# A list scheduler's table of durations is rewritten, and its rule for picking the next piece is widened

## The chip, the cores and the metric

The kernel runs on one core of one Trainium2 chip. The metric is device time in microseconds from one launch to its end, as the median of several executions. One further execution was taken with the hardware profiler; all rows below come from it.

## The reference

Two layers of an encoder over 1024 tokens of width 1024. In each layer one wide projection of `x` (1024 to 11520 columns) feeds three mixers, and their gated sum goes through an output projection and a layer norm:

```python
for l in range(DEPTH):
    h = jnp.einsum('bsd,dn->bsn', x, w_in[l]) + b_in[l]
    (u_a, z_a, p_b, z_b, q_c, k_c, v_c, z_c, g_a, g_b, g_c) = _split(h, SPLIT_SIZES)
    o_a = rwkv7_branch(u_a, z_a, ...)      # a recurrence over the tokens, 16 heads, both directions
    o_b = pool_branch(p_b, z_b, ...)
    o_c = attention_branch(q_c, k_c, v_c, z_c, cos, sin)
    merged = (sigmoid(g_a) * (o_a @ proj_a[l]) + sigmoid(g_b) * (o_b @ proj_b[l])
              + sigmoid(g_c) * (o_c @ proj_c[l]))
    x = _normalize(DEEPNORM_ALPHA * x + merged @ w_out[l], LN_EPS) * ln_g[l] + ln_b[l]
```

The recurrence of the first mixer is, for every head and token, `state = state * w + (state @ nkk) b + v k` with output `state @ r`. The kernel does it in chunks of 64 tokens, which turns it into small matrix products, a 64 by 64 triangular inverse for each chunk, and a chain from chunk to chunk.

## The kernel before, in words

**Dense work.** Every large product is done in float32 accuracy by splitting both operands into a high and a low part. One piece (`mm` in `Dense.make`) is three matmuls of 128x512 for one slice k of the sum: L584, L585 and L586, written "a dense triple" below. A tile of the projection is 8 slices times 2 halves of the tokens. A weight block of four slices is loaded by SP, cast to its high part by ScalarE (L552, `wh`) and split into its low part by GpSimd (L553, `wl`).

**The recurrent stage** (`rwkv`). Heads are worked off in 8 pairs j, each in 4 quarters q, so 32 quarters a layer. In a quarter, both directions of 4 chunks are prepared together:
- `prep` (`fac1` to `fac3`, `score`): scaled copies of keys and queries. `fac3` makes one half of `nk` on GpSimd (L965) and scales it on VectorE (L967, L968); `score` is L979 on TensorE, masked by VectorE (L982, L984).
- `inverse`: a serial chain of levels. Each is 16 or 32 small matmuls in quarters of the array (L1053), then one VectorE operation (`X`, L1085) and one ScalarE cast (`U`, L1086), on which the next level's matmuls wait. GpSimd makes a low part for it (L1065).
- `seq`: four steps a quarter, each A, then B, then C, and then the next step's A. A is L1142 and L1144 on TensorE, then `u` on VectorE (L1148); B is L1159, then two copies on ScalarE (`uv`, L1163); C is L1173 and L1178, then the state's update `sbd` (L1183) and an output copy `y` (L1188 or L1190) on VectorE.
- Further pieces: `nkt` (L1009), `av` (L1023), the low-rank products (`psl`, L911 and L912), the norm of the keys (`psk` L782, `psr` L824), the output norm (`psy`, L1244).

The attention stage transposes each v tile (`psv`, L1431) after ScalarE has evacuated it (`rawv`, L1367).

**What sets the order.** The whole program is written out in the order that a list scheduler (`Sched.run`) makes while the kernel is built. Each piece of work is a `Th` with a list of steps (engine, ns). The scheduler keeps a clock for each engine, works out for the next piece of each line when it could begin (`st`), and takes, of those that begin within `TOL` of the earliest, the one with the lowest `p`; `p` is a due time, or the place of the line. On TensorE a piece's `st` holds a margin `LATE` of 146 ns after its operands. Dense triples of the recurrent stage come from a `Feed`; they have the highest `p`, so they fill in, unless the scheduler's own account of the clock asks for them. Every engine runs its instructions in the order in which they are written, so this list alone decides who stands behind whom:

```python
st = r if e == "W" else max(ck[e], r + (HOPI + LATE if e == "P" else 0.0))
...
lim = min(c[0] for c in cand) + TOL
st, p, r, ln = min((c for c in cand if c[0] <= lim), key=lambda c: c[1])
```

The durations are never read on the chip. They only shape the order.

Of the kernel before, what the change touches and what calls it, by code (L numbers as in the profile page):

```python
# [20 lines left out]
DEPTH, S, D = 2, 1024, 1024  # L21
# [78 lines left out]
SLACK, RESERVE, LATE, TOL, BUB = 1112.0, 20000.0, 146.0, 26.0, 87.0  # L100
# [15 lines left out]
class Th:  # L116
# [4 lines left out]
    __slots__ = ("fn", "steps", "needs", "gives", "ring", "chain", "rows", "side", "hold", "drop", "tail", "gen", "due", "lag")  # L121

    def __init__(self, fn, steps, needs=(), gives=(), ring=(), chain=True, rows=0.5, side=(), hold=None, drop=None, tail=None, lag=0.0):
# [4 lines left out]
        self.due, self.lag = None, lag  # L128
# [8 lines left out]
class Feed:  # L137
# [10 lines left out]
    def work(self):  # L148
        return 640.0 * self.n
# [33 lines left out]
class Sched:  # L183
# [3 lines left out]
    def __init__(self):  # L187
# [6 lines left out]
        self.dense = False  # L194
        self.hist = []

    def pe(self, start, ns, rows):
# [5 lines left out]
        t = start + ns * f  # L203
# [37 lines left out]
    def step(self, ln, steps, t, rows):  # L241

        for ops in steps:
            end = 0.0
            for e, ns, more, early in ops:
# [3 lines left out]
                else:  # L249
                    x = max(x, self.clock[e])  # L250
                    y = self.pe(x, ns, rows) if e == "P" else x + ns
# [7 lines left out]
    def issue(self, ln, r):  # L259
# [22 lines left out]
        ln.t = self.step(ln, steps, ln.t, th.rows)  # L282
# [101 lines left out]
def trunk(ctx: ExitStack, tc: tile.TileContext, a: dict, out, dbg=None):  # L384
# [124 lines left out]
    class Dense:  # L509
# [56 lines left out]
        def make(self, src, nk, rhs, evac, halves=(0, 1), needs=(), gives=(), ev=(("A", 570.0),), key=None, ering=(), first=False):  # L566
# [62 lines left out]
    def rwkv(l):  # L629
        P = pc["P"]  # L630
        w_in = a["w_in"][l]
        with ExitStack() as es:
# [110 lines left out]
            def pair_uv(j):  # L743
                o = []

                def tr(o, tg):
# [3 lines left out]
                    def fn():  # L750
# [13 lines left out]
                return ([Th(tr(0, t0), [("P", 428.0), ("A", 530.0), ("A", 530.0)], needs=n0 + [("v", j)], ring=("m",), gives=[("uv0", j)])],  # L764
                        [Th(tr(1, t1), [("P", 428.0), ("A", 530.0), ("A", 530.0)], needs=n1, ring=("m",), gives=[("uv", j)])])
# [3 lines left out]
            def pair_kk(j):  # L769
# [73 lines left out]
                for g in range(2):  # L843
                    o += [Th(f2(g), [("A", 520.0)], needs=[("kt", j)], ring=("t",), hold=hold[g]),
                          Th(f4(g), [("P", 428.0), ("D", 660.0)], ring=("m",), drop=hold[g])]
                o.append(Th(f5, [("G", 3770.0)]))
# [45 lines left out]
            def prep(j, d, q):  # L892
# [96 lines left out]
                if q % 2 == 0:  # L989
# [4 lines left out]
                      Th(score, [("P", 980.0), ("D", 602.0), ("D", 602.0)], needs=ss, ring=("m", "m"), gives=[("sc", d, Q)])]  # L994
# [3 lines left out]
            def joint(j, q):  # L998
# [28 lines left out]
                return ([Th(nkt, [("P", 930.0), ("A", 500.0), ("A", 500.0)], needs=[("sc", d, Q) for d in range(2)], ring=("m", "m"), gives=[("nkt", Q)])],  # L1027
# [959 lines left out]
```

## Time and profile before

| | |
|---|---|
| Median of 3 runs | 4210.23 us (4204.23 to 4212.84) |
| The profiled execution | 4213.04 us, span of its instructions 4211.3 us |
| Mean granted TensorE clock | 0.984 of full |
| TensorE busy | 4072.7 us, 97% of the span |
| VectorE, ScalarE, GpSimd busy | 2358.1, 2057.1, 1650.8 us |
| Dense matmuls L584, L585, L586 on `xh` | 3136 each, mean 425, 395, 396 ns |

Matmuls are pipelined, so the time from one matmul's start to the next one's start is less than the duration that a row gives. Where the text speaks of a slot, it is that distance between starts.

### The profile page before, as it was taken

Reading aid. Unit: us, or ns where it says so; the run is one execution under the profiler, and the core shown is the slowest. Engines: PE = TensorE matmul, PEld = TensorE weight load, DVE = VectorE, ACT = ScalarE, POOL = GpSimd, SP = SyncE. Lnnn points to the kernel's source line nnn. Section 1 sums busy time; section 2 is a strip of 40 time slices with the busy share of each in tenths; the row PEclk is TensorE's granted clock in tenths of the full one; section 3 lists DMA queues with packets and bytes.
Section 4 is the critical chain, followed back from the end, with each engine's and each line's share of the span. In section 5 each row is a group of like instructions: output and inputs, shape, how many; then the busy total and the mean of one; then the engine's idle time right before and its main releaser. Section 6 shows DMA issues by size and latency. Waiting matters only on the chain. (4 is left out here: it accounts for less than half of the span.)

```text
span 4211.3 us, 118890 instructions
## 1 busy us (share of the span) xinstructions
PE 4072.7 (97%) x50808; PEld 3195.4 (76%) x50808; DVE 2358.1 (56%) x4361; ACT 2057.1 (49%) x4198; POOL 1650.8 (39%) x2498
## 2 busy tenths in 40 slices
PE   8999999999999999999989999999999999999998
PEld 6777777777777778877767777777777777788777
DVE  3766666565504555545647666665655046555455
ACT  5566666565523553322146666665655235533210
POOL 4344334443343333353243443444433333333532
PEclk9999999999999899999999999999999999999999
DMA  2111111111134333155311111111111343321553
GB/s 90 33 42 36 44 40 37 41 36 50 48 101 111 116 109 98 55 174 190 121 51 32 38 39 42 40 36 44 34 53 48 106 113 112 115 88 55 180 182 118
DMA packets 329185, 326.30 MB, mean 77 GB/s; under 512 B 23536, under 2 KB 264384, under 8 KB 328655
## 3 DMA queue, kind: packets, MB, share of 16 engines
q1 hardware_dynamic: 301551, 233.66, 18.7%
q0 software_dynamic: 27104, 85.04, 5.8%
q8 instruction: 398, 6.52, 0.6%
q14 instruction: 132, 1.08, 0.1%
HBM read 224.86 MB, written 81.99 MB: 73 GB/s over the span
## 5 line engine op out<-in xcount | busy, mean ns | idle before, releaser
L584 PE MATMUL psdn<-xh,wh 128*128 128x512 f32 x3136 | 1332.1, 425 | 12.6 <-ACT wh L552 10.5
L586 PE MATMUL psdn<-xh,wl 128*128 128x512 f32 x3136 | 1241.4, 396 | 8.4 <-POOL wl L553 7.9
L585 PE MATMUL psdn<-xl,wh 128*128 128x512 f32 x3136 | 1238.5, 395 | 0.0
L553 POOL TENSOR_TENSOR wl<-wr,wh 128x512 fp32r<-128x512 f32 (+1 forms) x436 | 587.3, 1348 | 1222.1 <-ACT wh L552 1212.0
L584 PEld LDWEIGHTS psdn<-xh,wh 128*128 128x128 f32 x3136 | 596.2, 190 | 174.0 <-issue 27.6
L586 PEld LDWEIGHTS psdn<-xh,wl 128*128 128x128 f32 x3136 | 595.2, 190 | 151.3 <-POOL wl L553 17.8
L585 PEld LDWEIGHTS psdn<-xl,wh 128*128 128x128 f32 x3136 | 598.3, 191 | 105.3 <-issue 6.9
L552 ACT CAST wh<-wr 128x512 fp32r<-128x512 f32 (+2 forms) x484 | 291.3, 602 | 674.9 <-PE psdn L585 279.6
L1085 DVE TENSOR_TENSOR X<-pst,c 128x512 f16<-128x512 f32 x320 | 219.7, 687 | 191.8 <-PE pst L1053 185.7
L1086 ACT CAST U<-pst 128x512 f16<-128x512 f32 x320 | 185.9, 581 | 95.2 <-PE pst L1053 91.8
L1183 DVE SCALAR_TENSOR_TENSOR sbd<-sqp,wc,sbd 128x64 f32<-128x64 f32 x480 | 114.2, 279 | 203.7 <-PE sqp L1178 179.1
L1163 ACT COPY uv<-sqp 64x128 f32<-64x128 f32 x512 | 133.0, 260 | 97.5 <-PE sqp L1159 87.8
L1152 ACT ACTIVATE sbd<-sbd,wc 128x64 f32<-128x64 f32 x480 | 140.9, 343 | 61.9 <-PE sqp L1144 61.6
L1065 POOL TENSOR_TENSOR nl<-sc,nh 64x512 f16<-64x512 f32 x128 | 156.2, 1220 | 16.9 <-ACT nh L1062 11.4
L979 PE MATMUL pssc<-ar,nk 64*64 64x128 f32 x4096 | 150.7, 274 | 1.5 <-ACT uv L759 1.4
L1148 DVE TENSOR_TENSOR u<-sqp,sc 128x128 f32<-128x128 f32 x256 | 73.8, 288 | 136.7 <-PE sqp L1144 78.7
L625 POOL DMA_DIRECT2D sga<-gt x96 | 54.1, 564 | 245.0 <-ACT gt L624 134.1
L965 POOL TENSOR_TENSOR nk<-ta,k 128x256 f32<-128x256 f32 x128 | 98.0, 766 | 132.0 <-ACT ta L958 128.4
L1053 PEld LDWEIGHTS <-X 64*64 64x64 f16 x6144 | 130.0, 110 | 23.2 <-DVE sc L984 6.4
L1159 PEld LDWEIGHTS sqp<-u,sc 64*64 64x64 f32 x2048 | 79.6, 133 | 82.5 <-issue 42.4
L1053 PEld LDWEIGHTS <-U 64*64 64x64 f16 x5120 | 112.6, 109 | 36.6 <-ACT uv L1163 13.7
L1053 PE MATMUL pst<-X,U 64*64 64x64 f16 x5120 | 137.3, 194 | 1.0 <-ACT U L1086 0.7
(717 smaller groups left out, 8021.4 us busy)
## 6 DMA issues: line engine op xcount, KB each, us to landing
wr<-in_w_in_dram SPq DMA_DIRECT2D x360, 256.0 KB, 3.0
sga<-gt POOLq DMA_DIRECT2D x96, 256.0 KB, 2.3
g<-sga SPq DMA_DIRECT2D x96, 256.0 KB, 4.4
wr<-in_proj_a_dram SPq DMA_DIRECT2D x64, 256.0 KB, 3.1
sza<-sz POOLq DMA_DIRECT2D x32, 256.0 KB, 3.6
bva<-bv POOLq DMA_DIRECT2D x32, 256.0 KB, 4.0
oa<-o POOLq DMA_DIRECT2D x32, 256.0 KB, 3.6
oat<-oa SPq DMA_DIRECT2D x32, 256.0 KB, 4.2
```

The source lines that it names most:

```text
L552: nc.scalar.copy(hi[:, 0:n, :], r[:, 0:n, :])
L553: self.lo.tensor_tensor(out=lo[:, 0:n, :], in0=r[:, 0:n, :], in1=hi[:, 0:n, :], op=ALU.subtract)
L584: nc.tensor.matmul(ps, lhsT=hi[:, kk, :], rhs=ah, start=(k == 0), stop=False)
L585: nc.tensor.matmul(ps, lhsT=hi[:, kk, :], rhs=al, start=False, stop=False)
L586: nc.tensor.matmul(ps, lhsT=lo[:, kk, :], rhs=ah, start=False, stop=(k == nk - 1))
L979: nc.tensor.matmul(ps[h][HS[h if x == 0 else 1 - h], c, :], lhsT=nk[HS[h], c, x, :], rhs=ar[HS[h], c].rearrange("p a t -> p (a t)"), start ...
L1053: nc.tensor.matmul(ps[hs, d, c], lhsT=l, rhs=r, start=start and d == 0 and c == 0, stop=stop, skip_group_check=True)
L1065: nc.gpsimd.tensor_tensor(out=nl[HS[h]], in0=sc[HS[h], :, :, h, 0:64], in1=nh[HS[h]], op=ALU.subtract)
L1085: tt(out=x, in0=ps[0], in1=mask(i + 1), op=ALU.mult)
L1086: nc.scalar.copy(L["U"], ps[1])
L1152: act(sbd[d], sbd[d], AF.Copy, scale=J["wc", d, Q % NB][:, pl[d][0]:pl[d][0] + 1])
L1163: nc.scalar.copy(uv[HS[h], two, h, :], pu[HS[h], 128:256].rearrange("p (s e) -> p s e", s=2))
```

## The change

Three things are changed in the scheduler's numbers; no operation of the kernel is added or taken away.

1. The durations of the pieces: a dense triple is booked at 690 ns instead of 640, the side work that it triggers at 520 ns on ScalarE instead of 307 and 1235 ns on GpSimd instead of 620, the matmuls of an inverse level at 560 instead of 1000 ns, and so on.
2. A piece can have a shape (`full`, `quarters`, `columns`, `rows`); the scheduler's TensorE clock takes `SWITCH` = 92 ns more when the shape differs from the piece before.
3. `TOL` is 200 ns instead of 26.

```diff
-SLACK, RESERVE, LATE, TOL, BUB = 1112.0, 20000.0, 146.0, 26.0, 87.0
+SWITCH, PROD = 92.0, 690.0
+SLACK, RESERVE, LATE, TOL, BUB = 1112.0, 20000.0, 146.0, 200.0, 87.0
...
-        t = start + ns * f
+        t = start + (ns + (SWITCH if shape != self.shape else 0.0)) * f
+        self.shape = shape
...
-                        out_.append(Th(mm(pi, kk, h), [("P", 640.0)],
-                                       side=(("A", 307.0), ("G" if self.lo is nc.gpsimd else "D", 620.0 if self.lo is nc.gpsimd else 335.0)) if kk == 0 and h == halves[0] else (),
+                        out_.append(Th(mm(pi, kk, h), [("P", PROD)],
+                                       side=(("A", 520.0), ("G" if self.lo is nc.gpsimd else "D", 1235.0 if self.lo is nc.gpsimd else 602.0)) if kk == 0 and h == halves[0] else (),
...
-                    inv.append(Th(levx(i), [("P", 1000.0), [("D", 690.0), ("A", 600.0)]] if i < 5 else [("P", 540.0), ("D", 690.0)], rows=RI))
+                    inv.append(Th(levx(i), [("P", 560.0), [("D", 602.0), ("A", 480.0)]] if i < 5 else [("P", 290.0), ("D", 602.0)], rows=RI, shape="quarters"))
```

The changed file is four lines longer, so its lines have numbers that are higher by 4 (L1148 becomes L1152). The order moves over the whole program. The places that the prediction speaks of are shown from it.

**TensorE, pair 6, first quarter, second step**, from the last dense matmul ahead of B to C. `sqp` is the step's PSUM tile, `u` what VectorE made after A, `uv` what ScalarE makes after B. Before (the left-out rows are two inverse levels, and the second dense triple):

```order
L586 MATMUL psdn<-xh,wl 128x512
L1159 MATMUL sqp<-u_17891,sc 64x64 x4
...
L584 MATMUL psdn<-xh,wh 128x512
L585 MATMUL psdn<-xl,wh 128x512
...
L1173 MATMUL sqp<-uv,nk 64x64 x4
L1178 MATMUL sqp<-uv,sc 64x64 x4
```

The same step in the changed order:

```order
L590 MATMUL psdn<-xh,wl 128x512
L1163 MATMUL sqp<-u_17205,sc 64x64 x4
L983 MATMUL pssc<-ar,nk 64x128 x16
L1177 MATMUL sqp<-uv,nk 64x64 x4
L1182 MATMUL sqp<-uv,sc 64x64 x4
L588 MATMUL psdn<-xh,wh 128x512
```

Between B and C there were two inverse levels and two dense triples; now there is one half of a score, and TensorE goes back to dense work only behind C.

**VectorE, the same place**, from the state update ahead of A to `u`. Before:

```order
L1183 SCALAR_TENSOR_TENSOR sbd_295<-sqp,wc,sbd_295 128x64
L1188 COPY y<-sqp 128x2x64
L967 SCALAR_TENSOR_TENSOR nk<-nk,cum 128x4x64
L968 TENSOR_TENSOR nk<-nk,cum 128x4x64
L1085 TENSOR_TENSOR X<-pst_17778,c_284 128x512
L1148 TENSOR_TENSOR u_17891<-sqp,sc 128x128
```

In the changed order the next `u` of that quarter stands so:

```order
L1187 SCALAR_TENSOR_TENSOR sbd_295<-sqp,wc,sbd_295 128x64
L1192 COPY y<-sqp 128x2x64
L988 TENSOR_TENSOR sc<-pssc,c_284 128x4x128
L950 TENSOR_TENSOR ar<-kk,lw 128x4x63
L953 TENSOR_TENSOR ar<-r,lw 128x4x64
L1152 TENSOR_TENSOR u_17324<-sqp,sc 128x128
```

Where `u` stood behind the scaling of `nk`, whose second instruction reads what GpSimd makes, it now stands behind a masked score and two products that GpSimd has no part in.

## Rows read from the trace of the kernel before

**Rows 1.** Busy time by stretch: us, engines, granted clock, DMA share, GB/s.

```profile
130.00:1160.00 1030.00, 1022.22 (x20497) 785.73 (x20496) 656.31 (x1413) 649.88 (x1415) 423.02 (x804) 1.00 0.13 40
...
2235.00:3175.00 940.00, 927.81 (x18546) 712.74 (x18539) 614.94 (x1310) 600.54 (x1299) 394.53 (x760) 1.00 0.13 40
```

**Rows 2.** Waits of TensorE: us in total, times, longest us.

```profile
PE psr L824 <- ACT nx L797: 11.8, 2, 5.9
...
PE sqp L1159 <- DVE u L1148: 8.5, 9, 2.4
...
PE psv L1431 <- ACT rawv L1367: 3.6, 2, 2.0
```

**Rows 3.** Timeline of TensorE: start us, us, engine, line, operation.

```profile
601.30 0.39 PE L585 MATMUL psdn<-xl,wh 128*128 128x512 f32 x1
...
602.23 0.40 PE L586 MATMUL psdn<-xh,wl 128*128 128x512 f32 x1
602.56 0.44 PE L1053 MATMUL pst<-T,nh 64*64 64x64 f16 x16
...
604.33 0.50 PE L584 MATMUL psdn<-xh,wh 128*128 128x512 f32 x1
604.67 0.39 PE L585 MATMUL psdn<-xl,wh 128*128 128x512 f32 x1
...
609.64 0.22 PE L1144 MATMUL sqp<-sbd,ar 64*64 64x64 f32 x1
609.79 0.70 PE L871 MATMUL psb<-rk__10834,cst 128*128 128x512 f32 x1
```

**Rows 4.** Timeline of TensorE where only dense triples are left.

```profile
1194.80 0.39 PE L584 MATMUL psdn<-xh,wh 128*128 128x512 f32 x1
...
1203.41 0.39 PE L586 MATMUL psdn<-xh,wl 128*128 128x512 f32 x1
```

**Rows 5.** Timeline of VectorE, pair 6.

```profile
952.01 0.97 DVE L967 SCALAR_TENSOR_TENSOR nk<-nk,cum 128x256 f32<-128x256 f32 x1
955.66 0.43 DVE L968 TENSOR_TENSOR nk<-nk,cum 128x256 f32<-128x256 f32 x1 [2.68 <-POOL nk L965]
...
956.60 0.28 DVE L1148 TENSOR_TENSOR u<-sqp,sc 128x128 f32<-128x128 f32 x1
```

**Rows 6.** Timeline of GpSimd, same stretch.

```profile
952.77 1.36 POOL L553 TENSOR_TENSOR wl<-wr,wh 128x512 fp32r<-128x512 f32 x1
...
954.89 0.74 POOL L965 TENSOR_TENSOR nk<-ta,k 128x256 f32<-128x256 f32 x1
```

**Rows 7.** Timeline of TensorE, same stretch.

```profile
954.16 0.39 PE L586 MATMUL psdn<-xh,wl 128*128 128x512 f32 x1
956.94 0.45 PE L1159 MATMUL sqp<-u,sc 64*64 64x64 f32 x8 [2.40 <-DVE u L1148]
```

**Rows 8.** Busy time and granted clock (the figure ahead of the DMA share) just behind it.

```profile
957.60:961.00 3.40, 3.40 (x29) 2.30 (x24) 0.69 (x1) 0.94 (x3) 0.00 (x0) 0.51 0.09 34
```

**Rows 9.** Timeline of VectorE 40 us earlier.

```profile
914.86 1.38 DVE L967 SCALAR_TENSOR_TENSOR nk<-nk,cum 128x256 f32<-128x256 f32 x1
...
918.26 0.41 DVE L967 SCALAR_TENSOR_TENSOR nk<-nk,cum 128x256 f32<-128x256 f32 x1
```

**Rows 10.** Timeline of GpSimd, same stretch.

```profile
914.62 2.64 POOL L1065 TENSOR_TENSOR nl<-sc,nh 64x512 f16<-64x512 f32 x2
```

**Rows 11.** Groups of instructions, 130 to 1160 us: xcount, busy us, mean ns, idle before.

```profile
L1085 DVE TENSOR_TENSOR X<-pst,c 128x512 f16<-128x512 f32 x160 | 109.9, 687 | 96.4 <-PE pst L1053 93.3
```

**Rows 12.** Timeline of ScalarE in the attention stage.

```profile
1433.99 1.15 ACT L1367 ACTIVATE rawv<-psdn,pc 128x512 f32<-128x512 f32 x1 [0.68 <-PE psdn L586]
```

**Rows 13.** Timeline of TensorE, same stretch.

```profile
1433.56 0.39 PE L586 MATMUL psdn<-xh,wl 128*128 128x512 f32 x1
1433.79 0.60 PE L1493 MATMUL pspt<-cst,s 128*128 128x128 f32 x4
...
1435.37 0.66 PE L1431 MATMUL psv<-cst,rawv 128*128 128x128 f32 x4
```

More of the change, by code (lines that the diff above doesn't have):

```diff
@@ L116, with __init__ @@
 class Th:
-    __slots__ = ("fn", "steps", "needs", "gives", "ring", "chain", "rows", "side", "hold", "drop", "tail", "gen", "due", "lag")
-    def __init__(self, fn, steps, needs=(), gives=(), ring=(), chain=True, rows=0.5, side=(), hold=None, drop=None, tail=None, lag=0.0):
+    __slots__ = ("fn", "steps", "needs", "gives", "ring", "chain", "rows", "side", "hold", "drop", "tail", "gen", "due", "lag", "shape")
+    def __init__(self, fn, steps, needs=(), gives=(), ring=(), chain=True, rows=0.5, side=(), hold=None, drop=None, tail=None, lag=0.0, shape="full"):
         self.fn, self.needs, self.gives, self.ring, self.chain, self.rows = fn, tuple(needs), tuple(gives), tuple(ring), chain, rows
@@ L194, in __init__, with pe @@
         self.dense = False
+        self.shape = "full"
         self.hist = []
-    def pe(self, start, ns, rows):
+    def pe(self, start, ns, rows, shape):
         if not self.warm and self.cols(start - 2 * TICK, start) > 2 * COLDOK:
@@ L239, in ready, with step @@
         return r
-    def step(self, ln, steps, t, rows):
+    def step(self, ln, steps, t, rows, shape):
         for ops in steps:
@@ L250, in step @@
                     x = max(x, self.clock[e])
-                    y = self.pe(x, ns, rows) if e == "P" else x + ns
+                    y = self.pe(x, ns, rows, shape) if e == "P" else x + ns
                     self.clock[e] = y + more if e != "S" else x + 0.2 * ns
@@ L281, in issue @@
         p0 = max(ck["P"], ln.t)
-        ln.t = self.step(ln, steps, ln.t, th.rows)
+        ln.t = self.step(ln, steps, ln.t, th.rows, th.shape)
         if LOG is not None:
@@ L1026, in av @@
                     nc.scalar.copy(sc[:, :, :, 1, 0:64], ps)
-                return ([Th(nkt, [("P", 930.0), ("A", 500.0), ("A", 500.0)], needs=[("sc", d, Q) for d in range(2)], ring=("m", "m"), gives=[("nkt", Q)])],
-                        [Th(av, [("P", 930.0), ("A", 500.0)], needs=[("nt", Q), ("uv" if q in (1, 2) else "uv0", j)], ring=("m",), gives=[("av", Q)])])
+                return ([Th(nkt, shape="quarters", steps=[("P", 990.0), ("A", 500.0), ("A", 500.0)], needs=[("sc", d, Q) for d in range(2)], ring=("m", "m"), gives=[("nkt", Q)])],
+                        [Th(av, shape="quarters", steps=[("P", 950.0), ("A", 500.0)], needs=[("nt", Q), ("uv" if q in (1, 2) else "uv0", j)], ring=("m",), gives=[("av", Q)])])
             def place(d, q, i):
@@ L1517, in unit @@
                 nd = [("parts", ct, u)] if g < 2 else [("rope", "q", ct), ("rope", "k", ct)]
-                return [Th(t1, [("P", 860.0 if g == 2 else 436.0), ("D", 600.0)], needs=nd, ring=("m",), gives=[("t1", ct, u, h)]),
-                        Th(t2, [("D", 602.0), ("A", 800.0)]), Th(t3, [("P", 428.0), ("A", 478.0)]),
-                        Th(t4, [("P", 432.0), ("D", 200.0)], needs=[("vt", ct)] if first else (), gives=[("attu", ct, h, u)] + ([("att", ct, h)] if last else []))]
+                return [Th(t1, [("P", 460.0 if g == 2 else 1240.0), ("D", 600.0)], shape="rows" if g == 2 else "full", needs=nd, ring=("m",), gives=[("t1", ct, u, h)]),
+                        Th(t2, [("D", 602.0), ("A", 800.0)]), Th(t3, [("P", 490.0), ("A", 478.0)]),
+                        Th(t4, [("P", 890.0), ("D", 200.0)], needs=[("vt", ct)] if first else (), gives=[("attu", ct, h, u)] + ([("att", ct, h)] if last else []))]
             def combine(t):
@@ L1919, in token @@
                 if not last:
-                    o += [Th(back(g), [("P", 428.0), ("A", 480.0), ("D", 602.0)], ring=("m",)) for g in range(2)]
+                    o += [Th(back(g), [("P", 490.0), ("A", 480.0), ("D", 602.0)], ring=("m",)) for g in range(2)]
                 return d, o
```

30 lines of the change are left out of this document (15 added, 15 removed).

## The prediction

> **What bounds the kernel now.** The busy time by stretch comes first: in both recurrent stretches TensorE is busy for 1022.2 of 1030 and 927.8 of 940 us at full clock, while VectorE is busy for 656.3 and 614.9 us [rows 1]. So what the recurrent stage takes is what TensorE's instructions take in their order, plus 7.8 and 12.2 us of idle time. A new order can gain there in three ways only: by fewer changes of the array's shape, by a quicker pace of the same matmuls, and by shorter waits. The list of TensorE's waits says what the idle time is [rows 2]: of the seq chain, B waits for `u` 9 times, 8.5 us in all; at the start of each layer the key norm's second product waits 5.9 us for ScalarE; in attention the transposes of v wait for `rawv`. The timelines then give the prices. Outside the recurrent stage the work is nearly all dense, and its order hardly moves.
>
> **What a change of shape costs.** A dense matmul's slot is 0.2325 us in the mixture: four slots from 601.30 to 602.23 [rows 3]. The last dense matmul ahead of an inverse level takes 0.33 us, so 0.10 more. Coming back, the first dense matmul takes 0.34 (604.33 to 604.67), 0.11 more, and the last small matmul ahead of another shape holds its place for 0.15 us (609.64 to 609.79), where its neighbours take some 0.03. A trip from the whole array to small matmuls and back thus costs 0.10 + 0.12 + 0.11 = 0.33 us beyond the work itself.
>
> The scheduler does not weigh this price against anything: it books it on its clock after the choice is made. So I count the changed order. TensorE leaves dense work 876 times before and 752 times now, which looks like much. But transposes and low-rank products use the whole array too, and many of the trips that vanish led only to these. From whole-array work to small matmuls there are 750 changes before, 718 now: 32 x 0.33 = 10.6 us less. Changes between quarters (A, B, levels) and columns (C) rise from 220 to 274, as in the step shown, where C follows a score: 54 x 0.12 = 6.5 us more, with the holding time above as their price. The net is 4 us; with the transposes' own exits it may be 7. I take **-5 us**.
>
> **Pace.** Between the first A and the last C of a layer 642 dense triples are written before and 526 now; the 116 that are put off stand behind the recurrence, where only dense work is left. There a slot is (1203.41 - 1194.80) / 38 = 0.2266 us [rows 4] against 0.2325 [rows 3]. 2 layers x 116 x 3 x 0.0059 = **-4 us**. No other work hides behind these triples, and none is needed there.
>
> **The waits for `u`.** In pair 6 VectorE runs L967 at 952.01, then stands 2.68 us until GpSimd has made `nk` at L965, and only then comes `u`, which had nothing to wait for [rows 5]. GpSimd was late because L553 took 1.36 us ahead of it [rows 6], which the scheduler had booked at 0.62. TensorE waited 2.40 us for `u` [rows 7], and in the 3.4 us behind that its granted clock was 0.51, the lower of its two levels, 1.2 GHz [rows 8]: about 1.7 us more. The change books L553 at 1.235 us. In the order the effect shows: of 255 `u`, 75 have a scaling of `nk` (L967 or L968) between the output copy and themselves before, 27 now. I scale the 8.5 us by that: 8.5 x 48/75 = 5.4, with the 1.7 us of clock **-7 us**. The bounds are nothing and 8.5 + 1.7 = 10. The TensorE work that covers the seq chain also grows at its thin end: less than 0.6 us between A and B in 68 places before, 8 now; less than 0.9 us between B and C in 38, now none; less than 0.6 us between C and the next A in 42, now 2.
>
> **The start of a layer.** Between the key norm's first and second products on TensorE stand now 6 dense triples and one low-rank product instead of 4 triples, 2 x 0.70 us and the product, about 2 us more cover for the 5.9 us; but the two halves of the second product, which had 6 triples between them, stand side by side, and the second needs a ScalarE copy that the first one must be through for. Between 0 and -4 us for both layers; I take **-1 us**.
>
> **Attention.** From the end of the v tile's last slot (1433.79) to its transposes (1435.37) it takes 1.58 us [rows 13], since the evacuation starts at 1433.99 and lasts 1.15 [rows 12]. Before, 1.6 us or more of TensorE work stand between in all 14 places that wait for it. Now 10 of 12 places have 0.8 to 1.15 us: the wider `TOL` lets transposes in earlier. 10 x 0.4 to 0.75 = 4 to 7.5 us, less what the shorter evacuations save; **+4 us**.
>
> **The inverse chain.** From one level's matmuls to the next lies a VectorE operation of 0.69 us [rows 11]; with hand-overs as around the evacuation above, 0.20 us ahead of it and 0.23 behind it [rows 12, 13], that makes an estimate of 1.1 us. The work between two levels is at least 1.9 us before; now 86 of the 576 gaps have less than 1.5, 12 of them less than 0.9. Most should just hold. Bounds: nothing, and 86 x 0.5 = 43 us if each came half a microsecond late. I take **+2 us**, near the lower one, as A to B with the thinnest cover of before shows no wait.
>
> **Sum.** -5 - 4 - 7 - 1 + 4 + 2 = -11 us. The profiled execution took 4213.0 us (1.7 around its span of 4211.3), so 4202; the median of the runs is 2.8 below it, so **4199 us**. Whatever differs by less than 0.2%, 8 us, is no change for this measurement.
>
> **Rivals.**
> *All waits of the recurrent stage vanish* (0.12). The durations booked now agree with the rows, and the idle time there is 7.8 + 12.2 = 20 us [rows 1]. Then -5 - 4 - 20 - 2 for the clock, with nothing added: 4180 us. Against it: the cover of the inverse chain is thinner than before.
> *The gain is eaten* (0.23). The thin covers of the inverse chain and the attention's transposes take 11 us more than I booked, some 0.13 us for each of the 86 gaps: 4210 us, no change.
> *Slower, by stretched VectorE operations* (0.19). L967 took 1.38 us while GpSimd ran two L1065 in 2.64 us, and 0.41 when it did not [rows 9, 10]. No booked duration knows of this. The recurrent stretch loses 232 triples in all, 80 us a layer, so VectorE's share there rises from 656.3/1030 = 64% to 69%, and GpSimd's with it. A level whose operation stands behind a stretched one is 0.97 us late, and the thin covers no longer take that up. The kernel becomes slower by over 8 us from (11 + 8) / 0.97 = 20 such meetings on; with half of the 86 it would be 4199 + 42 = 4241 us. For it speaks that the first pairs, with VectorE at two thirds, have hardly a wait only because their covers were thick.
> The Trainium skill (SBUF — State Buffer, Who interferes with whom) says why: a VectorE instruction with two SBUF inputs contends with a GpSimd instruction that reads SBUF, and the one that comes second is blocked for the other's whole instruction. The trace agrees, with 1.38 against 0.41 us [rows 9, 10]; by that rule alone, more overlap makes the changed order slower, which is this rival.
> *The change does nothing* is not a case: the order moves on every engine.
>
> **How the numbers follow.** My forecast, -4 to -22 us, has 0.46, of which 0.06 lies within 8 us of no change. Faster: 0.40 + 0.12 = 0.52. Same: 0.06 + 0.23 = 0.29. Slower: 0.19. The range for 8 in 10 cuts off the better part of the first rival below 4178 and the worse half of the third above 4226: **4178 to 4226 us**; the forecast's own is 4188 to 4206.
>
> **What would show it.** Right: the last C of each layer comes some 80 us earlier, with a dense stretch of about 150 us behind it; B's wait for `u` falls from 8.5 us to under 4; the wait of L1431 (there L1435) rises above 3.6; TensorE's idle time in the recurrent stretch stays under 20 us for both layers; mean dense slots do not grow. Wrong: a new wait of L1053 (there L1057) for `X` of more than 10 us in all; L967 and L968 with means that are clearly longer; more stretches at the lower clock inside the recurrence, or a wait of dense triples for L553 behind it.

## The result, and the profile after

The changed kernel takes 4316.04 us (median, 4310.04 to 4324.92) where the kernel before, run beside it, takes 4211.53 (4204.23 to 4215.68). The ratio is 1.0251, with an interval of 1.0230 to 1.0273: it is slower by 105 us. I had forecast 4199 us and a range up to 4226.

The profiled execution has a span of 4310.1 us, 98.8 more than before. Busy time by stretch comes first. The columns are those of [rows 1]; the first row is the first recurrent stage, from the first A to the last C, the second the stretch from there to the output projection.

```profile
149.40:1143.00 993.60, 955.24 (x20080) 734.67 (x20079) 683.57 (x1411) 635.74 (x1387) 419.76 (x795) 0.98 0.12 36
1143.00:2014.70 871.70, 830.89 (x3761) 665.24 (x3760) 362.06 (x504) 307.25 (x565) 342.13 (x346) 0.97 0.38 117
```

The same two stretches of the kernel before:

```profile
152.90:1191.30 1038.40, 1030.62 (x20377) 789.77 (x20365) 648.45 (x1409) 644.03 (x1411) 430.69 (x822) 1.00 0.13 42
1191.30:1965.20 773.90, 744.58 (x3407) 599.29 (x3406) 362.76 (x504) 290.19 (x536) 299.54 (x314) 0.97 0.40 121
```

The recurrent stage is 44.8 us shorter and its last C comes 48.3 us earlier (I had said 80), but it also holds fewer dense matmuls: 1579 instead of 1927, which are done later. At 0.2266 us each [rows 4] those are 78.9 us. For the same work the stage has therefore become 34.1 us longer. By the same reckoning the stretch behind it is 97.8 - 80.2 = 17.6 us longer. In layer 1 the two are 30.1 and 15.0 us. Together they are 96.8 of the 98.8 us; the rest lies at the starts of the layers and in the output projections. "Loss" below always means a stage's duration against before, less 0.2266 us for each dense matmul that it has more.

TensorE idles for 38.4 us in that recurrent stage, where it idled for 7.8. VectorE is busy for 35 us longer with the same number of instructions, 1411 against 1409: its operations have become longer. TensorE's waits over the whole span say for whom it waits (total, times, longest, in us):

```profile
PE sqp L1146 <- DVE sbd L1187: 31.1, 30, 2.1
PE psdn L588 <- ACT rawv L1371: 22.9, 8, 4.4
PE psy L1248 <- POOL ysq L1243: 20.1, 14, 2.8
PE pspt L1497 <- ACT s L1489: 18.4, 10, 4.3
...
PE psr L828 <- ACT nx L801: 7.1, 4, 2.7
PE pst L1057 <- DVE X L1080: 6.0, 8, 1.0
...
PE sqp L1163 <- DVE u L1152: 3.1, 4, 1.0
...
PE psv L1435 <- ACT rawv L1371: 0.4, 2, 0.2
```

The same in the kernel before, for the waits that [rows 2] does not have:

```profile
PE pspt L1493 <- ACT s L1485: 3.3, 2, 1.7
...
PE psdn L584 <- ACT rawv L1367: 1.4, 2, 0.7
...
PE pst L1053 <- DVE X L1076: 0.9, 2, 0.5
...
PE sqp L1142 <- DVE sbd L1183: 0.2, 1, 0.2
```

Set against [rows 2]: the wait of B for `u` has fallen from 8.5 to 3.1 us and that of the key norm from 11.8 to 7.1, as forecast. The largest wait was hardly there before. A, the first product of a step, waits for the state's update `sbd`, 30 times, 31.1 us in all instead of 0.2. That is over half of the 56.2 us of idle time that the two recurrent stages gained; the next is the output norm's product `psy`, which waits 17.5 us there for GpSimd, 0.4 before.

One of the longest shows how. TensorE, from C (L1182) to the next A (L1146):

```profile
405.94 0.40 PE L1182 MATMUL sqp<-uv,sc 128*64 128x64 f32 x8
406.28 0.65 PE L1248 MATMUL psy<-cst,ysq 128*128 128x128 f32 x4
407.90 0.44 PE L1057 MATMUL pst<-X,nh 64*64 64x64 f16 x16 [0.97 <-DVE X L1080]
...
410.67 0.33 PE L1146 MATMUL sqp<-sbd,ar 64*64 64x64 f32 x2 [2.08 <-DVE sbd L1187]
```

VectorE at the same time:

```profile
404.29 1.38 DVE L972 TENSOR_TENSOR nk<-nk,cum 128x256 f32<-128x256 f32 x1
405.60 1.65 DVE L685 SCALAR_TENSOR_TENSOR v<-raw,pc,v 128x512 f32<-128x512 f32 x1
407.17 0.68 DVE L1080 TENSOR_TENSOR X<-pst,c 128x512 f16<-128x512 f32 x1
407.77 2.65 DVE L685 SCALAR_TENSOR_TENSOR v<-raw,pc,v 128x512 f32<-128x512 f32 x2
410.34 0.47 DVE L1187 SCALAR_TENSOR_TENSOR sbd<-sqp,wc,sbd 128x64 f32<-128x64 f32 x2
```

And GpSimd:

```profile
404.05 2.65 POOL L1069 TENSOR_TENSOR nl<-sc,nh 64x512 f16<-64x512 f32 x2
406.78 1.60 POOL L557 TENSOR_TENSOR wl<-wr,wh 128x512 fp32r<-128x512 f32 x1
...
409.12 0.74 POOL L969 TENSOR_TENSOR nk<-ta,k 128x256 f32<-128x256 f32 x1
```

C is through by 406.34, but the update begins at 410.34. VectorE works without a pause for all of these 4 us; it is behind. The first L685, a product of the token shift (before: L681), takes 1.65 us beside GpSimd's L1069, and two more, the one beside L557 and the other in part beside L969, take 2.65. The scheduler books 0.663 for each. L972 took 1.38 us; [rows 9] shows 0.41 as the undisturbed length of its neighbour of the same size. TensorE then pays a second time. Busy time and granted clock (the figure ahead of the DMA share) of the 3 us with the wait, and just behind them:

```profile
408.00:411.00 3.00, 0.92 (x34) 0.67 (x33) 3.00 (x6) 0.59 (x1) 1.83 (x3) 1.00 0.56 160
411.00:414.40 3.40, 3.34 (x87) 3.28 (x87) 1.56 (x5) 1.11 (x4) 0.00 (x0) 0.50 0.15 55
```

Behind the wait the clock stands at 0.50, that is 1.2 instead of 2.4 GHz. The recurrent stages have 30.7 us each at that clock, before 3.4 and nothing.

The groups of VectorE between 130 and 1160 us (count, busy us, mean ns). After:

```profile
L972 DVE TENSOR_TENSOR nk<-nk,cum 128x256 f32<-128x256 f32 x60 | 38.1, 635 | 7.9 <-POOL nk L969 7.9
...
L971 DVE SCALAR_TENSOR_TENSOR nk<-nk,cum 128x256 f32<-128x256 f32 x60 | 34.6, 576 | 0.0
...
L685 DVE SCALAR_TENSOR_TENSOR v<-raw,pc,v 128x512 f32<-128x512 f32 x28 | 31.9, 1163 | 4.1 <-ACT v L678 4.1
L685 DVE SCALAR_TENSOR_TENSOR r<-raw,pc,r 128x512 f32<-128x512 f32 x28 | 28.8, 1058 | 0.0
```

Before:

```profile
L968 DVE TENSOR_TENSOR nk<-nk,cum 128x256 f32<-128x256 f32 x61 | 32.2, 527 | 38.6 <-POOL nk L965 38.6
L967 DVE SCALAR_TENSOR_TENSOR nk<-nk,cum 128x256 f32<-128x256 f32 x61 | 30.7, 503 | 0.0
...
L681 DVE SCALAR_TENSOR_TENSOR v<-raw,pc,v 128x512 f32<-128x512 f32 x28 | 25.4, 935 | 1.8 <-ACT v L674 1.8
...
L681 DVE SCALAR_TENSOR_TENSOR r<-raw,pc,r 128x512 f32<-128x512 f32 x28 | 20.6, 742 | 0.0
```

The scheduler books all of these the same in both kernels. By the trace of the first recurrent stage, 61 of 80 products of the token shift now spend at least 0.1 us beside a GpSimd operation that reads a tile, before 28 of 78. Of the scalings of `nk` no more do so, 59 of 118 against 68 of 120, but for longer, 41 us in all against 35.

The second loss is in the attention stage. Dense triples wait for the evacuation of a v tile: they need its PSUM buffer. TensorE at the longest such wait:

```profile
1409.86 0.39 PE L590 MATMUL psdn<-xh,wl 128*128 128x512 f32 x1
1414.62 0.79 PE L588 MATMUL psdn<-xh,wh 128*128 128x512 f32 x1 [4.38 <-ACT rawv L1371]
```

ScalarE, which evacuates it:

```profile
1411.74 0.83 ACT L1417 CAST ks<-rawk 64x256 fp32r<-64x256 f32 x2 [5.72 <-DVE rawk L1396]
1412.59 0.82 ACT L1419 CAST ks<-rawk 64x256 fp32r<-64x256 f32 x2
1413.43 2.07 ACT L1371 ACTIVATE rawv<-psdn,pc 128x512 f32<-128x512 f32 x2
```

ScalarE stands still for 5.72 us in front of a cast that needs the rotated keys, and the evacuation is queued behind it. A second wait for ScalarE there has grown too: that of `pspt` for `s`, from 3.3 to 18.4 us over the span.

### The profile page after: what moved, and what is told of

Read it like the earlier page. It is cut to its first block, busy times and chain, and to the rows that moved or that the text cites. A ratio compares the mean times of both kernels' runs of the same rounds, so it can differ in the third digit from the quotient of the medians.

```text
span 4310.1 us, 119015 instructions
## 1 busy us (share of the span) xinstructions
PE 4093.1 (95%) x50808; PEld 3212.1 (75%) x50808; DVE 2418.5 (56%) x4361; ACT 2070.0 (48%) x4198; POOL 1706.6 (40%) x2498
## 3 DMA queue, kind: packets, MB, share of 16 engines
q1 hardware_dynamic: 301551, 233.66, 18.3%
## 5 line engine op out<-in xcount | busy, mean ns | idle before, releaser
L557 POOL TENSOR_TENSOR wl<-wr,wh 128x512 fp32r<-128x512 f32 (+1 forms) x436 | 615.5, 1412 | 1128.4 <-ACT wh L556 1108.4
L588 PEld LDWEIGHTS psdn<-xh,wh 128*128 128x128 f32 x3136 | 596.8, 190 | 186.9 <-ACT rawv L1371 26.2
L1089 DVE TENSOR_TENSOR X<-pst,c 128x512 f16<-128x512 f32 x320 | 219.7, 687 | 163.9 <-PE pst L1057 160.3
L1389 DVE TENSOR_TENSOR rawq<-rawq,cos 128x1024 f32<-128x1024 f32 x12 | 20.8, 1730 | 341.0 <-DMA rot<-rawq 341.0
L1069 POOL TENSOR_TENSOR nl<-sc,nh 64x512 f16<-64x512 f32 x128 | 164.3, 1283 | 28.0 <-ACT nh L1066 23.1
L1146 PEld LDWEIGHTS sqp<-sbd,ar 64*64 64x64 f32 x2048 | 91.6, 134 | 94.0 <-DVE sbd L1187 37.5
L1146 PE MATMUL sqp<-sbd,ar 64*64 64x64 f32 x2048 | 128.8, 231 | 31.6 <-DVE sbd L1187 31.1
L969 POOL TENSOR_TENSOR nk<-ta,k 128x256 f32<-128x256 f32 x128 | 101.9, 802 | 125.1 <-ACT ta L962 122.7
L628 ACT ACTIVATE gt<-psdn,pc 128x512 f32<-128x512 f32 x96 | 66.1, 689 | 171.0 <-PE psdn L590 146.6
```

The costliest lines, as they stand in the source:

```text
L557: self.lo.tensor_tensor(out=lo[:, 0:n, :], in0=r[:, 0:n, :], in1=hi[:, 0:n, :], op=ALU.subtract)
L588: nc.tensor.matmul(ps, lhsT=hi[:, kk, :], rhs=ah, start=(k == 0), stop=False)
L1069: nc.gpsimd.tensor_tensor(out=nl[HS[h]], in0=sc[HS[h], :, :, h, 0:64], in1=nh[HS[h]], op=ALU.subtract)
L1089: tt(out=x, in0=ps[0], in1=mask(i + 1), op=ALU.mult)
L1146: nc.tensor.matmul(pu[HS[h], 64 * d:64 * d + 64], lhsT=ar[HS[h], c, 0, :], rhs=sbd[d][HS[h]], start=d == 0, stop=True, skip_group_check=True)
```

## The experiments

All results, as worked out from the traces of each run. "Idle" is TensorE's in the recurrent stage of layer 0 and layer 1. The losses are per layer (0 and 1), in us. Ratios are to the kernel before, run on the same chip. Idle and losses are of the one profiled execution, which can lie off the median (e4: 4311.82 against 4298.31 us), so small differences between runs say little there.

| Run | Median us (before) | Ratio, interval | Idle | Loss, recurrent | Loss behind it |
|---|---|---|---|---|---|
| before | 4211.53 | 1 | 7.8, 12.6 | 0 | 0 |
| changed | 4316.04 (4211.53) | 1.0251, 1.0230 to 1.0273 | 38.4, 38.2 | 34.1, 30.1 | 17.6, 15.0 |
| e1_tol26 | 4261.59 (4205.14) | 1.0130, 1.0114 to 1.0145 | 21.5, 22.1 | 12.7, 10.1 | 14.8, 11.2 |
| e2_tol200 | 4230.92 (4205.14) | 1.0054, 1.0039 to 1.0069 | 23.7, 23.5 | 16.5, 12.3 | -1.6, -3.2 |
| e3_levels_old | 4367.23 (4205.14) | 1.0381, 1.0353 to 1.0409 | 47.0, 46.8 | 50.0, 45.6 | 19.5, 22.3 |
| e4_side_old | 4298.31 (4205.14) | 1.0213, 1.0196 to 1.0230 | 37.2, 34.8 | 26.2, 20.5 | 26.8, 30.4 |
| e5_recurrent_only | 4228.76 (4211.22) | 1.0038, 1.0024 to 1.0052 | 16.7, 16.6 | 7.3, 3.0 | -4.1, -4.1 |
| e6_attention_only | 4232.42 (4211.22) | 1.0046, 1.0031 to 1.0061 | 7.9, 11.2 | -0.3, -0.4 | 4.5, 10.7 |
| e7_dense_only | 4255.27 (4211.22) | 1.0099, 1.0084 to 1.0114 | 24.2, 24.0 | 26.8, 21.5 | -8.0, -9.9 |
| e8_switch_only | 4271.97 (4211.22) | 1.0143, 1.0128 to 1.0159 | 34.3, 35.0 | 36.6, 32.3 | -4.4, -10.3 |
| e9_after_memset | 4163.19 (4209.51) | 0.9896, 0.9879 to 0.9912 | 10.2, 10.0 | -14.2, -18.7 | 0.7, 2.5 |
| e10_before_memset | 4135.89 (4209.51) | 0.9829, 0.9812 to 0.9845 | 4.1, 5.7 | -7.7, -10.5 | -22.4, -17.7 |
| e11_dense645 | 4245.47 (4209.51) | 1.0085, 1.0069 to 1.0101 | 18.4, 18.5 | 15.8, 12.0 | -5.1, -4.0 |
| e12_tol30 | 4227.17 (4209.51) | 1.0045, 1.0030 to 1.0060 | 19.4, 21.0 | 14.1, 12.5 | -11.9, -6.0 |
| e13_attention_old | 4279.55 (4212.09) | 1.0155, 1.0140 to 1.0170 | 38.5, 37.6 | 34.4, 27.2 | -0.3, 4.1 |
| e14_three_memsets | 4197.64 (4212.09) | 0.9961, 0.9946 to 0.9976 | 21.6, 22.7 | 2.7, -0.6 | 4.6, 3.6 |
| e15_late150 | 4213.51 (4212.09) | 1.0003, 0.9993 to 1.0012 | 10.4, 15.3 | 3.2, 7.6 | -9.7, -2.1 |
| e16_lo_on_vector | 4227.23 (4212.09) | 1.0035, 1.0022 to 1.0048 | 7.7, 12.1 | -0.8, -0.2 | 2.8, 7.3 |
| e17_dense_late | 4203.50 (4210.72) | 0.9978, 0.9968 to 0.9988 | 7.7, 12.2 | -2.2, 1.8 | -5.5, -9.1 |
| e18_switch_late | 4216.37 (4210.72) | 1.0007, 0.9997 to 1.0016 | 8.0, 12.0 | -0.3, 0.3 | 0.3, 1.9 |

### Which half of the change: e1 to e4

Two theories: the wider choice (W), or the booked durations (D).

```diff
 # e1, on the changed kernel
-SLACK, RESERVE, LATE, TOL, BUB = 1112.0, 20000.0, 146.0, 200.0, 87.0
+SLACK, RESERVE, LATE, TOL, BUB = 1112.0, 20000.0, 146.0, 26.0, 87.0
 # e2, on the kernel before
-SLACK, RESERVE, LATE, TOL, BUB = 1112.0, 20000.0, 146.0, 26.0, 87.0
+SLACK, RESERVE, LATE, TOL, BUB = 1112.0, 20000.0, 146.0, 200.0, 87.0
```

> The changed kernel with TOL back at 26, all booked durations and SWITCH as changed. Theory W (the wider choice is the cause: with TOL 200 the dense triples between the first A and the last C of a layer fall from 642 to 526, and VectorE's long products L685 come to stand ahead of the state update): this order has 648 triples there, so the idle time of TensorE in the first recurrent stage falls from 38 us to under 15 and the time to 4195 to 4235 us. Theory D (the shorter booked durations of the inverse levels thin the covers whatever TOL is): it stays above 4270 us, with A still waiting for sbd by over 8 us a layer.

> The kernel before with TOL 200 alone; durations and shapes are the old ones. Its order has 538 triples a layer in the recurrent stage and 42 places where an L681 stands between the critical operations of VectorE ahead of a state update (before 10, changed 44). Theory W: 4270 to 4320 us, A waits for sbd by some 15 us a layer. Theory D: 4200 to 4225 us, as before.

Both theories fall: e1 lies between their ranges and e2 below that of W and above that of D. Each half alone is slower, by 56 and 26 us, and together they are slower by more than the sum. The losses behind the recurrent stage appear in e1 and not in e2, so these come from the numbers and not from `TOL`.

```diff
 # e3, on the changed kernel (lev0, newt1 and newt2 likewise back to the old numbers)
-inv.append(Th(levx(i), [("P", 560.0), [("D", 602.0), ("A", 480.0)]] if i < 5 else [("P", 290.0), ("D", 602.0)], rows=RI, shape="quarters"))
+inv.append(Th(levx(i), [("P", 1000.0), [("D", 690.0), ("A", 600.0)]] if i < 5 else [("P", 540.0), ("D", 690.0)], rows=RI, shape="quarters"))
 # e4, on the changed kernel
-side=(("A", 520.0), ("G" if self.lo is nc.gpsimd else "D", 1235.0 if self.lo is nc.gpsimd else 602.0))
+side=(("A", 307.0), ("G" if self.lo is nc.gpsimd else "D", 620.0 if self.lo is nc.gpsimd else 335.0))
```

> The changed kernel with the old booked durations of the inverse chain (lev0, levx, newt1, newt2) and everything else as changed, TOL 200. Theory D: the thick covers come back, 4210 to 4245 us, idle in the first recurrent stage under 15 us. Theory W: the order has 486 triples in the recurrent stage, still fewer, so it is as slow as the changed kernel or slower, 4290 to 4340 us.

> The changed kernel with the old booked durations of the weight block's cast and split (ScalarE 307, GpSimd 620, VectorE 335), everything else as changed, TOL 200. Theory W: little changes, 4295 to 4330 us. Theory S (the side work, now booked at its true length, is what shifts the attention stage, where 15 us a layer were lost): 4275 to 4295 us, with the attention stage's idle time back at some 30 us a layer and the recurrent stage as in the changed kernel.

To undo the levels makes it worse still, above the range of either theory, and the waits for `X` grow, from 7.2 to 24.1 us, where theory D had them go. In the changed kernel those 7.2 us are all that the thinner cover of the inverse chain, on which I had booked the risk, costs by its own waits. Theory S falls too, by the time and by the place: with the old side work the loss behind the recurrent stage grows, and only the recurrent stage gains some.

### One part of the numbers alone: e5 to e8

Each on the kernel before, with `TOL` 26.

```diff
 # e5: inverse chain, A, B, C, score, nkt, av and the norms as in the change, for example
-inv.append(Th(levx(i), [("P", 1000.0), [("D", 690.0), ("A", 600.0)]] if i < 5 else [("P", 540.0), ("D", 690.0)], rows=RI))
+inv.append(Th(levx(i), [("P", 560.0), [("D", 602.0), ("A", 480.0)]] if i < 5 else [("P", 290.0), ("D", 602.0)], rows=RI))
 # e6: t1, t3, t4 and the transposes of v as in the change, for example
-return [Th(t1, [("P", 860.0 if g == 2 else 436.0), ("D", 600.0)], needs=nd, ring=("m",), gives=[("t1", ct, u, h)]),
+return [Th(t1, [("P", 460.0 if g == 2 else 1240.0), ("D", 600.0)], needs=nd, ring=("m",), gives=[("t1", ct, u, h)]),
 # e7: the dense piece 640 -> 690, its side work 307, 620, 335 -> 520, 1235, 602
 # e8: shapes, and SWITCH 0 -> 92
```

> The kernel before with the new booked durations of the recurrent stage's pieces alone (inverse chain, A, B, C, score, nkt, av, the norms); TOL 26, no SWITCH, dense and attention durations old. Theory D (the levels booked at 560 instead of 1000 are what thins the covers): the recurrent stage takes the loss of the run with TOL 26, 10 to 14 us a layer more than before, with 15 us of idle time in the first recurrent stage or more, and the attention stage stays as before: 4225 to 4240 us. Theory M (no single number does it; the old numbers were a set): under 8 us of loss, 4200 to 4215 us. The order has 704 triples in the recurrent stage (before 642) and 44 places with an L685 ahead of a state update (before 10).

> The kernel before with the new booked durations of the attention pieces alone (t1, t3, t4, the transposes of v); the recurrent stage keeps its order. Theory A (the attention's loss of 15 us a layer comes from its own durations, t1 at 1240 instead of 436 and t4 at 890 instead of 432, which move dense triples away from behind them): 4225 to 4245 us, with waits of dense triples or of pspt on ScalarE in the attention stage above 20 us. Theory S (it comes from the dense piece and its side work): within 8 us of before.

> The kernel before with the dense piece at 690 and its side work at 520, 1235 and 602 alone. Theory S: the attention stage takes 10 us a layer more, 4220 to 4240 us. Theory A: within 8 us of before, or a little faster where L557 and L557's neighbours on GpSimd are now expected at their true length (idle of B for u falls).

> The kernel before with shapes and SWITCH 92 alone. By the prediction's first term a clock that books the switch should save a few us: 4195 to 4210 us. Rival: the scheduler's clock runs slower against the other engines' clocks, so it puts fewer triples (616 instead of 642) as cover, and the covers come out thin: 4215 to 4240 us, with A waiting for sbd.

Every part alone makes the kernel slower, by 18, 21, 44 and 61 us. That sums to 144 us, where e1, which has them all, loses 56. So they cannot be priced one by one. Only e6 came out as one of its theories said. e5 lies in the range of theory D, but with a loss of 7.3 and 3.0 us in the recurrent stages where it said 10 to 14. e7 and e8 are slower than any range that I gave them; e7 is faster behind the recurrent stage, where theory S had it slower. `SWITCH`, which I had counted as the part with the gain, costs most by itself, all of it in the recurrent stage: there B waits for `u`, and not, as the rival had it, mainly A for `sbd`:

```profile
PE sqp L1163 <- DVE u L1152: 24.9, 21, 2.9
```

In e6 only the stage behind the recurrence is slower, as theory A said; its rows name the same two waits as the changed kernel:

```profile
PE pspt L1497 <- ACT s L1489: 10.5, 7, 2.4
PE psdn L588 <- ACT rawv L1371: 10.2, 5, 2.8
```

### Is it the stretching? e9, e10 and e14

Here GpSimd's two largest operations read nothing from SBUF any more, while the scheduler's numbers stay, and with them the order. The low parts become zero, so these kernels leave that part of the computation out.

```diff
-self.lo.tensor_tensor(out=lo[:, 0:n, :], in0=r[:, 0:n, :], in1=hi[:, 0:n, :], op=ALU.subtract)
+if self.lo is nc.gpsimd:
+    for _ in range(2):      # 3 in e14
+        nc.gpsimd.memset(lo[:, 0:n, :].bitcast(F32), 0.0)
...
-nc.gpsimd.tensor_tensor(out=nl[HS[h]], in0=sc[HS[h], :, :, h, 0:64], in1=nh[HS[h]], op=ALU.subtract)
+for _ in range(2):          # 3 in e14
+    nc.gpsimd.memset(nl[HS[h]], 0.0)
```

> The changed kernel in the same scheduler's numbers, but GpSimd's two largest operations, L557 (wl) and L1069 (nl), are each replaced by two memsets of the same tile, which read no SBUF: the low parts are zero, so that part of the computation is left out, while the order of every engine and GpSimd's load stay about the same. Theory C (VectorE operations with two inputs are stretched by GpSimd's reads, L685 from 0.66 to 1.3 us and more, and this is what makes the thin covers fail): the mean of L685 falls from 1059 to under 800 ns, the idle time of the first recurrent stage from 38 to under 18 us and the time by 30 us or more, more than the kernel before gains by the same edit. Theory Q (it is where L685 stands in VectorE's queue, at whatever length): the idle time stays above 28 us.

> The control: the kernel before with the same two operations replaced by two memsets each (the low parts are zero and that part of the computation is left out). Theory C: it gains little, as its recurrent stages have 7.8 and 12.6 us of idle time, so 4185 to 4210 us. Theory Q says the same; what tells is how much more the changed kernel gains.

> As the run of the changed kernel with two memsets in place of each L557 and L1069, but with three (low parts zero, that part of the computation left out), so that GpSimd is busy for longer than in the changed kernel itself: 1.59 us against 1.42 for wl, and 3 x 2 x 0.52 = 3.1 us against 2.57 for nl. Theory C (what matters is that GpSimd's reads stretch VectorE's operations): L685 stays near 0.76 us, the idle time of the first recurrent stage under 20 us, the recurrent stage under 960 us. Theory G (what matters is that GpSimd came free earlier): idle above 30 us there and the recurrent stage back at 980 us or more.

The recurrent stage of layer 0 in e9 (changed order, two memsets):

```profile
139.30:1084.70 945.40, 935.19 (x20080) 720.99 (x20080) 628.30 (x1411) 631.71 (x1387) 376.51 (x918) 1.00 0.12 38
```

In e10 (order of before, two memsets):

```profile
147.00:1177.60 1030.60, 1026.51 (x20373) 788.35 (x20361) 619.89 (x1409) 643.37 (x1411) 392.18 (x961) 1.00 0.14 42
```

In e14 (changed order, three memsets):

```profile
137.50:1099.80 962.30, 940.67 (x20080) 725.21 (x20080) 629.09 (x1411) 631.88 (x1387) 439.96 (x1048) 0.99 0.12 37
```

The changed kernel gains 153 us by the edit, the kernel before 74. VectorE's busy time in the stage falls by 683.57 - 628.30 = 55 us in the changed order and by 648.45 - 619.89 = 29 us in that of before. So the change had nearly doubled the time that VectorE loses to these two operations. With it gone, the changed order is ahead in the recurrent stage, -14.2 against -7.7 (layer 1: -18.7 against -10.5). Behind that stage it is not: 0.7 and 2.5 against -22.4 and -17.7. As a whole e9 is still 27 us slower than e10, where the changed kernel was 105 us slower than that of before. The loss in the attention stage is therefore not owed to these meetings; in e9 its waits for `rawv` and `s` are still 18.3 and 17.8 us. I had also expected the control to gain little, 4185 to 4210 us; at 4136 it shows that the kernel before paid for the two operations as well. In e9 the products of the token shift are back near their length without a disturbance:

```profile
L689 DVE SCALAR_TENSOR_TENSOR v<-raw,pc,v 128x512 f32<-128x512 f32 x28 | 21.0, 777 | 4.1 <-ACT v L682 4.1
L689 DVE SCALAR_TENSOR_TENSOR r<-raw,pc,r 128x512 f32<-128x512 f32 x28 | 20.0, 744 | 0.0
```

With three memsets GpSimd is busy for longer than in the changed kernel, 440 against 420 us, so most of the gain is not owed to its earlier freedom: of the 48.3 us that e9 won in this stage, 31.4 stay. VectorE stays at 629 us, and A's wait for `sbd` is 0.9 us where it was 31.1. The stage keeps 2.7 of its 34.1 us of loss. Duration and idle time, 962.3 and 21.6 us, stand just past the bounds I had given theory C (960 and 20); the largest wait that is left is one for GpSimd itself:

```profile
PE psy L1253 <- POOL ysq L1248: 33.9, 18, 2.9
...
PE sqp L1151 <- DVE sbd L1192: 0.9, 2, 0.5
```

One reserve: a memset also has no wait for ScalarE's cast ahead of it, so the runs take away that dependence with the contention; and the order of before was not run with three. That the low parts are zero does not show in TensorE's clock: in the first recurrent stage it is granted 1.00 in e10 as in the kernel before.

### The attention stage: e13 and e16

```diff
 # e13, on the changed kernel
-return [Th(t1, [("P", 460.0 if g == 2 else 1240.0), ("D", 600.0)], shape="rows" if g == 2 else "full", needs=nd, ring=("m",), gives=[("t1", ct, u, h)]),
+return [Th(t1, [("P", 860.0 if g == 2 else 436.0), ("D", 600.0)], shape="rows" if g == 2 else "full", needs=nd, ring=("m",), gives=[("t1", ct, u, h)]),
 # likewise t3 and the transposes of v 490 -> 428, t4 890 -> 432
 # e16, on the kernel before
+dn.lo = nc.vector
 attention(l, och, ocl, gr)
```

> The changed kernel with the old booked durations of the attention pieces (t1, t3, t4, the transposes of v), all else as changed. Theory A (the attention's loss of 15 us a layer is made by these durations): the wait of dense triples for rawv falls from 22.9 us to under 6 and the time by 20 to 36 us, to 4280 to 4297 us. Theory A2 (TOL 200 and the other new numbers do it as well): under 12 us are won.

> The kernel before with the split of the weight blocks (wl) on VectorE instead of GpSimd from the attention stage on, as it already is in the projections behind it. If GpSimd's reads also cost in the attention stage (with memsets the kernel before won 22 us a layer there), the wait for wl and the stretched operations go and it takes 4180 to 4205 us; if VectorE, which was busy half of the time there, becomes the one that is late, 4215 to 4250 us.

e13 wins 36 us against the changed kernel, by the medians. The loss behind the recurrent stage is gone in layer 0 and 4.1 us in layer 1. The wait for `rawv` falls by half only, not to under 6 us as theory A had it; that of `pspt` falls by 14 us:

```profile
PE psdn L588 <- ACT rawv L1371: 10.9, 4, 4.4
...
PE pspt L1497 <- ACT s L1489: 4.3, 4, 1.4
```

e16 is slower, as its second case said. VectorE is busy for half of the stretch behind the recurrent stage there, 388 of 777 us in layer 0, so whether it is VectorE that is late or the new order that costs stays open.

### Numbers that stand for nothing: e11, e12 and e15

```diff
 # e11
-out_.append(Th(mm(pi, kk, h), [("P", 640.0)],
+out_.append(Th(mm(pi, kk, h), [("P", 645.0)],
 # e12: TOL 26.0 -> 30.0      e15: LATE 146.0 -> 150.0
```

> The kernel before with the dense piece booked at 645 instead of 640 ns in the Feed's pieces, nothing else: a change of the numbers that stands for nothing. Theory R (the order of before is a favourable draw: any shift of the scheduler's clock deals the meetings on VectorE and GpSimd anew, and costs some 10 to 60 us as each part of the change did alone): 4222 to 4260 us. Theory N (the parts cost because of what they say): within 8 us of before. The order has 674 triples in the recurrent stage and 30 places with an L681 ahead of a state update (before 642 and 10).

> The kernel before with TOL 30 instead of 26, nothing else; its order too moves over the whole program (664 triples in the recurrent stage, 16 places with an L681 ahead of a state update). Theory R: 4215 to 4260 us. Theory N: within 8 us of before.

> The kernel before with LATE 150 instead of 146, nothing else: a third shift that stands for nothing. Its order stays nearest to that of before (640 triples in the recurrent stage, 12 places with an L681 ahead of a state update; before 642 and 10). Theory R: 4212 to 4250 us, the smaller loss the nearer the order. Theory N: within 8 us of before.

Two of three shifts that say nothing about the chip cost 36 and 18 us, as much as whole parts of the change. The third leaves the time as it was; its recurrent stages lose 3.2 and 7.6 us, and the stretches behind them win that back. VectorE's busy time in the recurrent stage goes some way to tell them apart (third pair of columns). e11:

```profile
153.20:1229.10 1075.90, 1057.52 (x20524) 805.95 (x20523) 674.12 (x1412) 647.90 (x1418) 434.79 (x833) 1.00 0.14 42
```

e15:

```profile
154.80:1195.00 1040.20, 1029.76 (x20367) 788.81 (x20359) 645.01 (x1409) 643.92 (x1411) 430.36 (x822) 1.00 0.13 41
```

With about the same 1410 instructions VectorE is busy for 648 us in the order of before and 645 in that of e15. In the other orders with GpSimd's reads and a new recurrent stage (changed, e1 to e5, e7, e8, e11, e12) it is 659 to 684, and all of these lose there. Within that group the relation is loose: e7 loses 26.8 us at 659, e5 7.3 at 671. How often operations meet is not all; it matters in front of whom.

### Only behind the recurrent stage: e17 and e18

```diff
 # e17, on the kernel before; the old numbers come back ahead of merge
+dn.num = (690.0, 520.0, 1235.0, 602.0)   # the dense piece and its side work
 attention(l, och, ocl, gr)
 # e18, on the kernel before; likewise SWITCH 92 and the shapes
```

> The kernel before, with the new durations of the dense piece (690) and of its side work (520, 1235, 602) from the attention stage to the projections only; the recurrent stage and the merge are scheduled with the old numbers. The run with these durations everywhere lost 27 us in each recurrent stage but took 8 and 10 us less than before, for the same number of dense triples, from the last C to the output projection. If numbers that say the truth help where VectorE and GpSimd are not near their limit: 4190 to 4204 us, faster than both kernels. Theory R (that gain was a draw too, and the stage's beginning deals it anew): 4205 to 4230 us.

> The kernel before, with SWITCH 92 and the shapes from the attention stage to the projections only; the recurrent stage and the merge are scheduled as before. The run with SWITCH everywhere lost 37 us in the recurrent stage but took 4 and 10 us less than before in the stages behind it, for the same number of triples. If it helps there: 4192 to 4206 us. Theory R: 4207 to 4230 us.

e17 beats the kernel before by 7 us or 0.22%, with an interval of 0.12 to 0.32%: clear of zero, though less than the 8 us that I had called no change. Its recurrent stage is that of before, and the stretch behind it is 5.5 and 9.1 us shorter:

```profile
155.40:1191.60 1036.20, 1028.52 (x20377) 788.87 (x20365) 648.63 (x1409) 642.65 (x1411) 429.85 (x822) 1.00 0.13 42
1191.60:1960.00 768.40, 736.82 (x3405) 592.79 (x3406) 368.19 (x504) 289.09 (x535) 298.26 (x314) 0.98 0.41 122
```

For `SWITCH` (e18) what it had gained there in e8 did not come back. One order each cannot say that the true numbers of the dense piece are better there; e17 is one better order.

## Why the prediction was wrong

- **Changes of shape and pace (-5 and -4): right, and more than that.** Of the 34.1 us of loss in the first recurrent stage, 30.6 are idle time more than before, and 27.3 us more at half the clock cost another 13.7. That is 44.3, so by subtraction the rest of the stage gained 10.2 us; in layer 1 it is 10.8. That makes 21 us for what I had at 9. The memset runs bear the size out: idle time aside, the two recurrent stages of e9 are 25 us shorter for the same work than those of e10. Shape and pace are not told apart by this.
- **The waits for `u` (-7): right in size.** 8.5 us became 3.1; I had 5.4 less. That it is the true length of L553 in the table which does this is not shown: e1 and e7 book it the same, and there B waits 11.1 and 20.1 us for `u`. What I had counted from the changed order itself held; that this order was a kind one in this respect is luck.
- **The start of a layer (-1): right in sign.** The wait of L828 fell by 4.7 us for both layers, a little more than my bound of 4.
- **The inverse chain (+2): right by its own wait, but the wrong place.** The waits for `X` (L1080 and L1089) are 7.2 us in all, from 0.9. The chain that failed was the other one, from C by way of `sbd` to A. I had counted its cover as grown, "less than 0.6 us between C and the next A in 42, now 2". That count has TensorE's work alone. What stands in VectorE's queue ahead of the update, and how long it takes beside GpSimd, was not in it. This is the step that failed, and the largest: I had put this chain's wait at nothing, and it is 31.1 us of the 56.2 us of new idle time. With the other new waits and the clock, the two recurrent stages lost 85 us; less the 21 us above they are 64 us longer for the same work.
- **Attention (+4): the sign right, the size and place wrong.** It is 32.6 us, counted to the output projections. The transposes of v that I had watched wait for 0.4 us, less than before. The dense triples wait in their place, for a PSUM buffer whose evacuation stands on ScalarE behind a cast that itself waits. I had followed the queue of TensorE and not that of ScalarE. In e13 all but 3.8 us of it go with the attention's old durations; by themselves, in e6, the new ones make 15.2. About 23 of the 32.6 us are idle time by the traces, and what the others are stays open.
- **The third rival** named the right mechanism for the recurrent stage, and e9, e10 and e14 bear it out there. Two signs that I had named for a wrong forecast came with it: longer means of L971 and L972, and more stretches at the lower clock. But I had tied it to the 86 thin covers of the inverse chain at 0.97 us each, and so, with half of them, to 4241 us; all 86 would have made 4282. The Trainium skill (SBUF — State Buffer, Who interferes with whom) restricts the contention to GpSimd instructions that read SBUF, and says that one that only writes does not contend. The trace agrees: with memsets that keep GpSimd as busy (e14), VectorE is 55 us less busy.
- **What I left out altogether** is the case that a new order costs by being new. Of the eleven other recurrent orders with GpSimd's reads that ran, none had less idle time than that of before, and shifts without meaning cost up to 36 us. I cannot say how much of the 105 us is such a loss and how much is owed to the new numbers; e1, e2 and e5 to e8 do not add up, so it can't be split. What can be given is what the two operations of GpSimd weigh in it: with memsets in their place the changed order is 27 us behind that of before instead of 105.

## What to carry to other kernels

When a list scheduler's order is changed, read the cover of a chain on every engine in its path: what stands in the queue ahead of the operation that closes the chain, and how long that takes when its neighbour engine is at work, not when it is alone. A number in such a table is not a measurement to be set right by itself; before any part of it is called good or bad, shift one number by an amount that means nothing and see what that alone costs. Here that price was 1 to 36 us, and all the gains that I had counted from the rows were 17 together.

## What was not expected of the hardware

An L685 beside GpSimd took 1.65 us, where those of `r` and `v` have means of 0.74 and 0.78 with memsets on GpSimd. Three of them and one `X` kept back an update of 0.28 us for 4 us. That `X`, which has one of its two inputs in PSUM, took 0.68 us beside L557, and none of the 64 of its line took more than 0.69. Two waits of TensorE, 0.97 and 2.08 us within 4 us, were followed by 3.4 us at half the clock, and such stretches made up 13.7 of a recurrent stage's 34.1 us of loss.
